# Output norms of a delta rule: the inverse root by Newton steps on GpSimd in place of a logarithm and an exponential on ScalarE

## The chip, the cores and the metric

The kernel runs on one core of one Trainium2 chip. The metric is the time of one execution on the device in microseconds (us), as the median of several runs. A core has five engines that run side by side, each through its own queue in order: TensorE (PE, the matrix multiplications; PEld is its loading of weights), VectorE (DVE), ScalarE (ACT), GpSimd (POOL), and SyncE (SP), whose queue here issues the loads of weights. Matmuls write into PSUM, everything else lies in SBUF.

## The reference, cut to what matters

The model is a trunk of two layers over 256 tokens of width 2048. Layer 0 is differential attention and a gated MLP with a short convolution, layer 1 a gated delta rule and another such MLP. The change lies in layer 1, where the output of the delta rule is normalised for every token and head, multiplied by a gate and projected:

```python
def rms_norm(x, g):
    xf = x.astype(jnp.float32)
    y = xf * lax.rsqrt(jnp.mean(xf * xf, axis=-1, keepdims=True) + RMS_EPS)
    return (y * g.astype(jnp.float32)).astype(x.dtype)

def gated_deltanet(h, w_in, conv_w, a_log, dt_bias, norm_g, w_out):
    ...
    o = gated_delta_rule(q, k, v, g, beta)       # (1, 256, 32 heads, 128)
    o = rms_norm(o, norm_g) * jax.nn.silu(z.reshape(b_sz, s_len, GDN_V_HEADS, GDN_HEAD_DIM).astype(jnp.float32))
    return o.reshape(b_sz, s_len, GDN_VALUE_DIM).astype(h.dtype) @ w_out
```

## The kernel before, in words

**Dense work.** Every projection is done by `dense` (or `dense_tok`, with tokens on the partitions). Weights come in chunks of 512 KB through `weights` (lines 81 to 91): SP issues the load into `raw`, ACT casts it to a rounded high part `whi` (line 89), DVE subtracts to get the low part `wlo` (line 90), and PE multiplies both parts (lines 151 and 152; a third product on line 154 where `wide` is false; lines 220 to 222 in `dense_tok`). Each of the three tiles has four slots. A plain chunk of `dense` is four tiles of the contraction times two tiles of outputs, so eight pairs of matmuls.

**Order of the work.** After each chunk `dense` calls `tick`, which lets every generator in the list `bg` run on to its next `yield`. Small work (keys, inverses, groups) is written as such generators, so that it stands between the chunks in the program. A `yield` means: one chunk later. The framework then plans the order of instructions on each engine over the whole program, with the program's order as priority and a model of their durations; the engines follow the planned queues in order, and semaphores keep the dependencies. Where `issue_after` or `add_manual_dep` stands, the order is bound by hand.

**The delta rule (`gdn`).** Four blocks of four key heads each. A block first projects its keys (`keys`, one generator a head), then one value head, the gates `z` (two calls of `dense_tok`, whose Silu goes into the tiles `zts`), then three more value heads; then comes the output projection of the block before it (`out`, eight calls of `dense` with two chunks each). After the last block its own output projection follows. `invert` and `levels` solve the triangular systems of a block, and for each of two groups of two key heads (four value heads) a generator `group` computes the outputs: so eight groups in all, two a block. Of these, the two of block 0 run while the keys of block 1 are made, and the others beside output projections.

**A group.** PE forms the products with the solved systems (line 773) into PSUM tiles of the pool `mp`, which has four banks. For each half `t` of the tokens an output tile `o` stays in PSUM; ACT squares it (line 796) and DVE adds up the squares for each token and head into `s`, 128 x 8 numbers (tile `os`, line 797). Then `lnexp` puts a load of ScalarE's table for logarithm and exponential on ACT's queue (line 297), bound behind the last sum, and `rsqrt` takes Ln and Exp of `s` (lines 316 and 317). DVE multiplies each `o` by its root and the gate (line 807). Three steps later PE transposes the products (line 818), and ACT and DVE write the high and low parts of `oc` (lines 821 and 822), four tiles of which feed the block's output projection.

**Neighbours.** `keys` uses the same helpers: PE sums its squares with a matrix of ones (line 329), its norms take Ln and Exp of a 128 x 512 tile and four exponentials of the decays, after a table load on line 297; `convs` takes a Silu, which needs another table (loads on line 593). The key step ends in eight copies on GpSimd into the tile `Cc` (line 652), which `invert` of that block reads. PE forms the products of keys and queries on lines 639 and 640 once DVE has scaled them (line 632).

Of the kernel before, what the change touches and what calls it, by code (L numbers as in the profile page):

```python
# [7 lines left out]

F32 = mybir.dt.float32
F32R = mybir.dt.float32r  # L10
AF = mybir.ActivationFunctionType
ALU = mybir.AluOpType
AX = mybir.AxisListType
# [3 lines left out]
P = 128  # L17
T = 256
D = 2048
KD = D // P  # L20
EPS = 1e-6
CK = 4
WARM = 7
LNEXP = "natural_log_exp_and_others"
# [2 lines left out]
class Trunk:  # L27
# [8 lines left out]
    def __init__(self, ctx, tc):  # L36
# [8 lines left out]
        self.mps = ctx.enter_context(tc.tile_pool(name="mps", bufs=4, space=PSUM))  # L45
        self.ones = self.cp.tile([P, P], F32, tag="ones", name="ones")
        nc.vector.memset(self.ones, 1.0)
        self.eps = self.cp.tile([P, 1], F32, tag="eps", name="eps")
        nc.vector.memset(self.eps, EPS)
        self.gx = self.cp.tile([P, KD + KD * T], F32, tag="x", name="x")  # L50
        self.x = self.gx[:, KD:].rearrange("p (k t) -> p k t", t=T)
        self.hs = self.cp.tile([P, KD * 2 * T], F32R, tag="h", name="h")
        self.h = self.rows(self.hs, KD)
        self.onesr = self.cp.tile([P, P], F32R, tag="onesr", name="onesr")
        nc.vector.tensor_copy(self.onesr, self.ones)
# [9 lines left out]
    def mp(self):  # L65
        return self.mps.tile([P, 512], F32, tag="mp", name="mp")

# [8 lines left out]
    def slots(self):  # L76

        return [self.wp.tile([P, CK * T], dt, tag=tag, name=tag, bufs=4)
                for tag, dt in (("raw", F32), ("whi", F32R), ("wlo", F32R))]

    def weights(self, ap, parts=1, slots=None, at=0):
# [5 lines left out]
        for i in range(parts):  # L87
            s = slice(i * n // parts, (i + 1) * n // parts)
            self.cast = nc.scalar.copy(hi[:, :, s], raw[:, :, s])  # L89
            nc.vector.tensor_tensor(lo[:, :, s], raw[:, :, s], hi[:, :, s].bitcast(F32), ALU.subtract)  # L90
        return hi, lo
# [9 lines left out]
    def dense_two(self, w, acts, done):  # L101

        nc = self.nc
        ps = [self.banks(), self.banks()]
        cut = KD - CK
        parts = [(c, (0, 1)) for c in self.firsts() if c[0] < cut] + [((cut, CK), (b,)) for b in range(2)]
        at = 0
# [24 lines left out]
    def dense(self, w, kt, acts, tiles=2, wide=True, each=None, apart=False):  # L132
# [5 lines left out]
        n = 2 * T if wide else T  # L138
        for k0, nk in self.chunks(kt, CK):
            hi, lo = self.weights(w[:, k0:k0 + nk, :])  # L140
# [66 lines left out]
    def dense_tok(self, w, kt, acts):  # L207
# [3 lines left out]
        ps = self.banks()  # L211
        for k0, nk in self.chunks(kt, CK // 2):
            hi, lo = self.weights(w[:, k0:k0 + nk, :])
# [52 lines left out]
    def norm_stat(self, wait=1, pool=None):  # L266
# [17 lines left out]
        m = self.sp.tile([P, T + 2], F32, tag="sq", name="ms", bufs=2)  # L284
        nc.vector.tensor_scalar(m, ps[:, :T + 2], 1.0 / D, EPS, ALU.mult, ALU.add)
        with self.lnexp(last):
# [26 lines left out]
    def rsqrt(self, out, ps, n):  # L313

        nc = self.nc
        nc.scalar.activation(out, ps, AF.Ln, bias=self.eps, scale=1.0 / n)
        nc.scalar.activation(out, out, AF.Exp, scale=-0.5)

    def split(self, out, a):

        self.nc.scalar.copy(out[:, 0], a)
        return self.nc.vector.tensor_tensor(out[:, 1], a, out[:, 0].bitcast(F32), ALU.subtract)
# [42 lines left out]
    def ffn(self, w_up, w_down, nj, cols_ap, done, final=False):  # L365
# [3 lines left out]
        with self.tc.tile_pool(name="fp", bufs=1) as fp:  # L369
# [3 lines left out]
            acts = []  # L373
            rows = self.rows(fp.tile([P, nj * 2 * T], F32R, tag="ac", name="ac"), nj)
            for j in range(nj):
# [17 lines left out]
    def attention(self, w_first, w_qk, w_v, w_o, nh, dist_ap, ident_ap, qg, kg, lvec, sub, start, done, lambda_init):  # L393

        nc, mp = self.nc, self.mp
        with self.tc.tile_pool(name="at", bufs=1) as at:
# [28 lines left out]
            def squares(r):  # L425
                sq = at.tile([P, 2, T], F32, tag="sq", name="sq", bufs=2)
                nc.scalar.square(sq, r)
                sp = at.tile([P, 2, 2, T], F32R, tag="sqp", name="sqp", bufs=3)
                self.split(sp, sq)
# [60 lines left out]
            def values(h, v, aT):  # L490
# [13 lines left out]
                for e in range(2):  # L504
                    on = at.tile([P, T], F32, tag="on", name="on", bufs=2)
                    nc.vector.scalar_tensor_tensor(
                        on, po[:, e * T:(e + 1) * T], subs[:, e:e + 1], ri[:, 0, :], ALU.mult, ALU.mult)
                    ac = at.tile([P, 2, T], F32R, tag=f"ac{h}_{e}", name="ac")
                    self.split(ac, on)
# [32 lines left out]
    def gdn(self, w_gate, w_in, w_z, w_out, nb, hb, gate_ap, const_ap, conv_col, ng, done):  # L542
# [7 lines left out]
        nc, tc, mp = self.nc, self.tc, self.mp  # L550
# [4 lines left out]
        with tc.tile_pool(name="gd", bufs=1) as gd:  # L555
# [204 lines left out]
            def group(gi, gr, lqs, done, vt, ready, zts, acts):  # L760

                TT = TTs[gi]
                n = 2 * len(gr)
                while gi not in done or len(ready) < len(gr):
                    yield
                sub = lqs[2 * gr[0]:2 * gr[-1] + 2]
                yield

                def prod(terms):
                    p = mp().rearrange("p (v c) -> p v c", c=P)  # L770
                    for v in range(n):
                        for i, (l, r) in enumerate(terms):
                            nc.tensor.matmul(p[:, v, :], l(v), r[:, v, :], start=i == 0, stop=i == len(terms) - 1)  # L773
                    return p[:, :n, :]

                w0 = gd.tile([P, gv, P], F32, tag="w0", name="w0", bufs=1)
                w1, r1 = vt[:, 0], vt[:, 1]
                nc.scalar.copy(w0[:, :n, :], prod([(lambda v: TT[:, 2 * v + 1, :], vt[:, 0])]))
                yield
                yield  # L780
                p = prod([(lambda v: sub[v][0][:, T:], w0)])
                nc.vector.tensor_tensor(r1[:, :n, :], r1[:, :n, :], p, ALU.subtract)
                yield
                yield
                nc.scalar.copy(w1[:, :n, :], prod([(lambda v: TT[:, 2 * v, :], r1)]))
                s = gd.tile([P, 2, gv], F32, tag="os", name="os", bufs=2)
                os = []
                for t in range(2):
                    if t == 0:
                        o = prod([(lambda v: sub[v][1][:, P:T], w0)])  # L790
                    else:
                        yield
                        yield
                        o = prod([(lambda v: sub[v][1][:, T:], w0), (lambda v: sub[v][1][:, :P], w1)])
                    sq = gd.tile([P, gv, P], F32, tag="qs", name="osq", bufs=2)
                    nc.scalar.square(sq[:, :n, :], o)
                    last = nc.vector.tensor_reduce(s[:, t, :n], sq[:, :n, :], AX.X, ALU.add)
                    os.append(o)
                with self.lnexp(last):
                    self.rsqrt(s[:, :, :n], s[:, :, :n], P)  # L800
                while gi not in zts:
                    yield
                ys = []
                for t in range(2):
                    y = zts[gi][:, t]
                    for v in range(n):
                        nc.vector.scalar_tensor_tensor(
                            y[:, v, :], os[t][:, v, :], s[:, t, v:v + 1], y[:, v, :], ALU.mult, ALU.mult)
                    ys.append(y)
                yield  # L810
                yield
                yield
                for v0 in range(0, n, 2):
                    p = mp()
                    for i in range(2):
                        for t in range(2):
                            a = i * T + t * P
                            nc.tensor.transpose(p[:, a:a + P], ys[t][:, v0 + i, :], ident)
                    oc = gd.tile([P, 2, 2, T], F32R, tag="oc", name="oc", bufs=hb)
                    pv = p.rearrange("p (v t) -> p v t", v=2)  # L820
                    nc.scalar.mul(oc[:, :, 0, :], pv, ng)
                    nc.vector.scalar_tensor_tensor(
                        oc[:, :, 1, :], pv, ng, oc[:, :, 0, :].bitcast(F32), ALU.mult, ALU.subtract)
                    acts += [oc[:, i] for i in range(2)]
# [10 lines left out]
            for b in range(nb):  # L835
# [5 lines left out]
                for op, i in plan + [("v", i) for i in range(1, hb)]:  # L841
# [7 lines left out]
                    elif op == "z":  # L849
# [3 lines left out]
                        for t in range(2):  # L853
                            nc.scalar.activation(zt[:, t].rearrange(flat), ps[:, t, :], AF.Silu,
                                                 scale=self.rstdc[:, t:t + 1])
# [83 lines left out]
def _layout(inputs):  # L939
# [13 lines left out]
    def blocks(w, kt, starts):  # L953
        w = w.reshape(kt, P, -1)
        return np.stack([np.concatenate([w[:, :, a:a + n] for a, n in s], 2) for s in starts]).transpose(0, 2, 1, 3)
# [25 lines left out]
    qk = blocks(x["diff_w_qkv"][0], KD, [[(T * (h + i), T)] for h in range(NH) for i in (0, NH)])  # L981
    two, cut = qk[:2], KD - CK

# [99 lines left out]
```

## Time and profile before

| what | value |
|---|---|
| runs | 2531.76, 2530.80 and 2531.91 us; median 2531.76 us |
| span of the profiled execution | 2530.1 us, 1.7 us below the median of the runs |
| granted TensorE clock | 1.000 |
| PE busy, PEld busy | 2520.0 and 2309.7 us |
| DVE, ACT, POOL busy | 1908.3, 1513.2 and 103.5 us |
| the stage of the delta rule | about 1060 to 1860 us of the span |

The span runs from the first to the last instruction of one profiled execution. For an engine, busy is the time with an instruction at work; matmuls overlap, so a busy PE is not one at its peak. In rows of the timeline the first number is the start in us from the span's start, the second the time in us that the row covers, then engine, line, operation, tiles (output <- inputs), shape and count; in brackets stands the idle time of the engine before it and what ended it. Rows of a line or tile give the shortest, median and longest duration in ns.

### The profile page before, as it was taken

Reading aid. Unit: us, or ns where it says so; the run is one execution under the profiler, and the core shown is the slowest. Engines: PE = TensorE matmul, PEld = TensorE weight load, DVE = VectorE, ACT = ScalarE, POOL = GpSimd, SP = SyncE. Lnnn points to the kernel's source line nnn. Section 1 sums busy time; section 2 is a strip of 40 time slices with the busy share of each in tenths; the row PEclk is TensorE's granted clock in tenths of the full one; section 3 lists DMA queues with packets and bytes.
Section 4 is the critical chain, followed back from the end, with each engine's and each line's share of the span. In section 5 each row is a group of like instructions: output and inputs, shape, how many; then the busy total and the mean of one; then the engine's idle time right before and its main releaser. Section 6 shows DMA issues by size and latency. Waiting matters only on the chain.

```text
span 2530.1 us, 41598 instructions
## 1 busy us (share of the span) xinstructions
PE 2520.0 (100%) x16151; PEld 2309.7 (91%) x16151; DVE 1908.3 (75%) x2847; ACT 1513.2 (60%) x2098; POOL 103.5 (4%) x197
## 2 busy tenths in 40 slices
PE   9999999999999999999999999999999999999999
PEld 8998899999999999998989989989999999999998
DVE  8886677777777555689788788788887777776544
ACT  7766656666666444485774675675566666665343
POOL 0000000000000000012021021021000000000000
PEclk9999999999999999999999999999999999999999
DMA  7555566666666666666455565555566666666775
GB/s 256 175 184 175 167 203 201 202 202 201 200 201 202 200 200 202 202 187 201 154 185 180 170 188 184 168 175 184 165 201 201 201 201 202 201 201 205 209 207 157
DMA packets 138199, 487.20 MB, mean 193 GB/s; under 512 B 15472, under 2 KB 18448, under 8 KB 138000
## 3 DMA queue, kind: packets, MB, share of 16 engines
q1 hardware_dynamic: 137712, 484.17, 60.8%
q8 instruction: 127, 2.08, 0.3%
q14 instruction: 72, 0.59, 0.1%
q10 hardware_dynamic: 288, 0.35, 0.0%
HBM read 482.32 MB, written 2.15 MB: 191 GB/s over the span
## 4 chain that ended last, share of the span: by engine, by line
PE 95%; ACT 3%; DVE 1%; issue 1%; DMA 0%; SPq 0%; ACTq 0%; DVEq 0%
PE ps L151 51%; PE ps L152 26%; PE ps L221 3%; PE ps L220 3%; PE ps L222 3%; PE mp L773 2%; PE mp L151 1%; PE ps L154 1%; ACT whi L89 1%; PE mp L329 1%; PE mp L152 0%; ACT L593 0%; ACT lt L631 0%; PE ps L123 0%; ACT L297 0%
## 5 line engine op out<-in xcount | busy, mean ns | idle before, releaser
L90 DVE TENSOR_TENSOR wlo<-raw,whi 128x1024 fp32r<-128x1024 f32 (+2 forms) x911 | 1104.1, 1213 | 506.1 <-ACT whi L89 498.2
L89 ACT CAST whi<-raw 128x1024 fp32r<-128x1024 f32 (+2 forms) x911 | 944.2, 1038 | 822.9 <-PE ps L151 657.0
L151 PE MATMUL ps<-h,whi 128*128 128x512 f32 (+1 forms) x4208 | 1369.4, 375 | 0.0
L152 PE MATMUL ps<-h,wlo 128*128 128x256 f32 x4208 | 1151.1, 274 | 1.0 <-DVE wlo L90 1.0
L151 PEld LDWEIGHTS ps<-h,whi 128*128 128x128 f32 x4208 | 796.1, 189 | 102.8
L152 PEld LDWEIGHTS ps<-h,wlo 128*128 128x128 f32 x4208 | 807.7, 192 | 2.8 <-DVE wlo L90 1.3
L151 PE MATMUL ps<-ac,whi 128*128 128x512 f32 x1546 | 506.8, 382 | 0.0
L152 PE MATMUL ps<-ac,wlo 128*128 128x256 f32 x1546 | 421.2, 273 | 0.0
L151 PEld LDWEIGHTS ps<-ac,whi 128*128 128x128 f32 x1546 | 292.1, 189 | 40.8 <-PE ps L151 0.2
L152 PEld LDWEIGHTS ps<-ac,wlo 128*128 128x128 f32 x1546 | 296.8, 192 | 0.1
L151 PE MATMUL ps<-oc,whi 128*128 128x512 f32 x512 | 170.7, 384 | 0.0
L220 PE MATMUL ps<-whi,h 128*128 128x512 f32 x384 | 146.5, 382 | 0.0
L221 PE MATMUL ps<-wlo,h 128*128 128x512 f32 x384 | 146.1, 380 | 0.0
L222 PE MATMUL ps<-whi,h 128*128 128x512 f32 x384 | 145.7, 379 | 0.0
L310 DVE SCALAR_TENSOR_TENSOR cv<-u,fcols,cv 128x255 f32<-128x255 f32 (+1 forms) x344 | 142.9, 477 | 0.0
L152 PE MATMUL ps<-oc,wlo 128*128 128x256 f32 x512 | 142.0, 277 | 0.0
L151 PEld LDWEIGHTS ps<-oc,whi 128*128 128x128 f32 x512 | 96.9, 189 | 12.5
L152 PEld LDWEIGHTS ps<-oc,wlo 128*128 128x128 f32 x512 | 98.3, 192 | 0.5
L308 ACT ACTIVATE cv<-u,fcols 128x256 f32<-128x256 f32 x172 | 93.9, 593 | 0.5 <-DVE u L205 0.5
L343 DVE TENSOR_TENSOR x<-ps,x 128x512 f32<-128x512 f32 x110 | 75.6, 687 | 12.5 <-PE ps L152 11.2
L310 DVE SCALAR_TENSOR_TENSOR cv<-u,cols,cv 128x255 f32<-128x255 f32 (+2 forms) x192 | 84.0, 486 | 0.3
L221 PEld LDWEIGHTS ps<-wlo,h 128*128 128x128 f32 x384 | 72.6, 189 | 10.0 <-DVE wlo L90 0.2
(220 smaller groups left out, 2077.3 us busy)
## 6 DMA issues: line engine op xcount, KB each, us to landing
raw<-w_up SPq DMA_DIRECT2D x344, 512.0 KB, 4.7
raw<-w_down SPq DMA_DIRECT2D x160, 512.0 KB, 3.8
raw<-w_in SPq DMA_DIRECT2D x128, 512.0 KB, 4.7
raw<-w_z SPq DMA_DIRECT2D x64, 512.0 KB, 3.7
raw<-w_out SPq DMA_DIRECT2D x64, 512.0 KB, 4.2
raw<-w_qk SPq DMA_DIRECT2D x56, 512.0 KB, 4.5
raw<-w_v SPq DMA_DIRECT2D x32, 512.0 KB, 3.5
raw<-w_o SPq DMA_DIRECT2D x32, 512.0 KB, 4.7
```

What stands on the lines that cost most here:

```text
L89: self.cast = nc.scalar.copy(hi[:, :, s], raw[:, :, s])
L90: nc.vector.tensor_tensor(lo[:, :, s], raw[:, :, s], hi[:, :, s].bitcast(F32), ALU.subtract)
L151: nc.tensor.matmul(bank[c][:, :n], hi[:, k, s], self.turns(a[:, :n // T, :]), start=first, stop=False)
L152: nc.tensor.matmul(bank[c][:, :T], lo[:, k, s], self.turns(a[:, :1, :]), start=False, stop=last and wide)
L154: nc.tensor.matmul(bank[c][:, :T], hi[:, k, s], self.turns(a[:, 1:, :]), start=False, stop=last)
L220: nc.tensor.matmul(ps[:, c, :], ah, wh, start=first, stop=False)
L221: nc.tensor.matmul(ps[:, c, :], ah, wl, start=False, stop=False)
L222: nc.tensor.matmul(ps[:, c, :], al, wh, start=False, stop=last)
L308: nc.scalar.activation(out, u, AF.Identity, bias=bias, scale=taps[n - 1])
L310: nc.vector.scalar_tensor_tensor(out[:, j:], u[:, :T - j], taps[n - 1 - j], out[:, j:], ALU.mult, ALU.add)
L343: self.nc.vector.tensor_tensor(x, part, x, ALU.add)
L773: nc.tensor.matmul(p[:, v, :], l(v), r[:, v, :], start=i == 0, stop=i == len(terms) - 1)
```

## The change

The group no longer calls `lnexp` and `rsqrt`. DVE forms the mean square plus epsilon, `m`, and a first guess of its inverse root from the bits of `m` read as an integer. Three Newton steps follow, with four operations each, all on GpSimd. The group then yields once before it goes on. The tiles `m`, `y` and `u` are new, 128 x 8 numbers each with two buffers. The row norms and the keys keep `lnexp` and `rsqrt`.

```diff
+I32 = mybir.dt.int32
+ROOT = float(0x5f3759df)
...
+    def root_steps(self, pool, s, scale):
+
+        nc = self.nc
+        m, y, u = (pool.tile(list(s.shape), F32, tag=f"rt{i}", name="rt", bufs=2) for i in range(3))
+        nc.vector.tensor_scalar(m, s, scale, EPS, ALU.mult, ALU.add)
+        nc.vector.tensor_scalar(y.bitcast(I32), m.bitcast(I32), -0.5, ROOT, ALU.mult, ALU.add)
+        for _ in range(3):
+            nc.gpsimd.tensor_tensor(u, y, y, ALU.mult)
+            nc.gpsimd.tensor_tensor(u, u, m, ALU.mult)
+            nc.gpsimd.tensor_scalar(u, u, -0.5, 1.5, ALU.mult, ALU.add)
+            nc.gpsimd.tensor_tensor(y, y, u, ALU.mult)
+        return y
...
-                    last = nc.vector.tensor_reduce(s[:, t, :n], sq[:, :n, :], AX.X, ALU.add)
+                    nc.vector.tensor_reduce(s[:, t, :n], sq[:, :n, :], AX.X, ALU.add)
                     os.append(o)
-                with self.lnexp(last):
-                    self.rsqrt(s[:, :, :n], s[:, :, :n], P)
+                s = self.root_steps(gd, s, 1.0 / P)
+                yield
                 while gi not in zts:
                     yield
```

## The prediction

> **What bounds the kernel now.** I read the page first, then the waits of TensorE, then the group's own tile, then the timelines around the eight groups.
>
> ```profile
> span 2530.1 us, 41598 instructions
> PE 2520.0 (100%) x16151; PEld 2309.7 (91%) x16151; DVE 1908.3 (75%) x2847; ACT 1513.2 (60%) x2098; POOL 103.5 (4%) x197
> PE 95%; ACT 3%; DVE 1%; issue 1%; DMA 0%; SPq 0%; ACTq 0%; DVEq 0%
> ```
>
> TensorE (PE) is busy throughout and is 95% of the chain that ended last; GpSimd (POOL) is nearly idle. The change touches no matmul, so it can move the time only by removing or making waits of PE. Those of the whole delta-rule stage, 1090 to 1855 us (header: engine line waited for, total, times, longest):
>
> ```profile
> PE mp L639 <- DVE cv L632: 1.4, 1, 1.4
> PE ps L152 <- DVE wlo L90: 1.0, 1, 1.0
> PE mp L329 <- ACT qp L321: 0.7, 2, 0.5
> PE mp L329 <- ACT whi L89: 0.5, 1, 0.5
> ```
>
> Together 3.6 us. That is the most a removed wait can give, against 5.06 us, 0.2% of 2531.76, which is about what a measurement of this kernel can tell from no change. Now the rows of the tile of sums `os`, and the table loads of line 297 (one for each norm or key step that takes a logarithm):
>
> ```profile
> L807 DVE SCALAR_TENSOR_TENSOR zt<-mp,os,zt x64: 336/340/351, 1239.2 to 1800.6; 128x128 f32<-128x128 f32 x64
> L316 ACT ACTIVATE os<-os,eps x8: 300/301/302, 1237.7 to 1796.4; 128x8 f32<-128x8 f32 x8
> L317 ACT ACTIVATE os<-os x8: 196/206/209, 1238.0 to 1797.5; 128x8 f32<-128x8 f32 x8
>   ACT os L317: 0.6, 1
> L297 ACT ACT_TABLE_LOAD  x28: 1283/1283/1283, 40.7 to 1860.1; - x28
> ```
>
> Eight groups, each with one load, one Ln and one Exp; their products (L807) found VectorE (DVE) idle for them once, for 0.6 us. Of the 28 loads 16 are the keys', 8 the groups', 4 the row norms'. I number groups (block, group); only (0,0) and (0,1) run beside the next block's keys, the other six beside output projections. The crowded place is (0,1); ACT, then DVE and PE there:
>
> ```profile
> 1258.40 1.28 ACT L297 ACT_TABLE_LOAD   x1 [1.10 <-DVE os L797]
> 1261.18 1.28 ACT L297 ACT_TABLE_LOAD   x1
> 1267.44 1.28 ACT L317 ACT_TABLE_LOAD   x1
> 1268.74 0.63 ACT L317 ACTIVATE qs<-qs 128x512 f32<-128x512 f32 x1
> 1257.69 0.68 DVE L797 TENSOR_REDUCE os<-osq 128x4 f32<-128x512 f32 x1
> 1261.97 2.15 DVE L807 SCALAR_TENSOR_TENSOR zt<-mp,os,zt 128x128 f32<-128x128 f32 x8
> 1264.04 1.21 DVE L90 TENSOR_TENSOR wlo<-raw,whi 128x1024 fp32r<-128x1024 f32 x1
> 1266.93 0.27 PE L152 MATMUL ps<-h,wlo 128*128 128x256 f32 x1
> 1270.14 0.49 PE L639 MATMUL mp<-cv 128*128 128x128 f32 x2 [1.41 <-DVE cv L632]
> ```
>
> PE's longest wait of the stage, 1.41 us, hangs on a key's exponential at 1268.74, behind an ACT queue that the group's load, Ln and Exp stand in.
>
> **The change part by part.** *ACT.* Removed per group: 1.283 + 0.301 + 0.206 = 1.79 us, 14.3 us over eight groups, and at 1258.40 the 1.10 us for which the load held the queue. In seven groups nothing on PE waits for it, so it is worth nothing there: ACT is 60% busy. At (0,1) it lies in the chain of the 1.41 us wait, and just ahead of the 0.5 us wait for a cast; I take both as gone, -1.9 us. Bounds: 0 (the key's own loads at 1261.18 and 1267.44 stay) and -3.6 us (every wait of the stage).
>
> *DVE.* Added: two operations on 128x8 per group, 16 in all. The nearest small row is 128x2:
>
> ```profile
> L476 DVE TENSOR_SCALAR l<-l,nlam 128x2 f32<-128x2 f32 x8 | 1.8, 228 | 0.3
> ```
>
> At 0.23 us each that is 0.46 us per group, 3.7 us in all, hidden under PE at DVE's 75%; uncovered, it is 3.7 us.
>
> *GpSimd.* Added: twelve dependent operations per group, 96 in all. The trace has no arithmetic on POOL; the nearest rows are its copies:
>
> ```profile
> L666 POOL COPY Ti<-half x8: 201/728/1212, 1105.7 to 1551.8; 128x16 f32<-128x16 f32 x8
> 1121.76 3.54 POOL L652 COPY Cc<-lt 32x64 f32<-32x64 f32 x8 [10.20 <-ACT lt L631]
> 1137.35 6.75 POOL L652 COPY Cc<-lt 32x64 f32<-32x64 f32 x8 [12.05 <-ACT whi L89]
> 1138.40 1.25 DVE L90 TENSOR_TENSOR wlo<-raw,whi 128x1024 fp32r<-128x1024 f32 x1
> 1140.22 3.72 DVE L90 TENSOR_TENSOR wlo<-raw,whi 128x1024 fp32r<-128x1024 f32 x3
> 1258.96 3.92 POOL L652 COPY Cc<-lt 32x64 f32<-32x64 f32 x8 [57.42 <-DVE lt L647]
> ```
>
> A small copy takes 0.20 us at its shortest. Eight others take 3.54 us (0.44 each) or, beside four weight subtractions (L90), 6.75 (0.84 each), so DVE's work slows POOL to about twice; L90 itself goes from 1.21 to 1.25. The bounds for a step are therefore 0.20 and 0.84 us, the chain of twelve 2.4 to 10.1 us. I take 0.33: small operands like the 0.20 row, with some of the slowing. Chain 4.0 us, with DVE's part 4.4.
>
> *The step of waiting.* `yield` hands on once, so products, transposes and `oc` come one weight chunk later. A chunk is eight pairs of matmuls; two consecutive pairs start at
>
> ```profile
> 1783.19 0.38 PE L151 MATMUL ps<-oc,whi 128*128 128x512 f32 x1
> 1783.52 0.38 PE L151 MATMUL ps<-oc,whi 128*128 128x512 f32 x1
> 1777.55 0.69 DVE L797 TENSOR_REDUCE os<-osq 128x4 f32<-128x512 f32 x1 [1.41 <-ACT osq L796]
> 1780.74 2.16 DVE L807 SCALAR_TENSOR_TENSOR zt<-mp,os,zt 128x128 f32<-128x128 f32 x8 [0.63 <-ACT os L317]
> 1784.07 0.27 PE L818 MATMUL mp<-con,zt 128*128 128x128 f32 x1
> 1784.01 1.21 DVE L90 TENSOR_TENSOR wlo<-raw,whi 128x1024 fp32r<-128x1024 f32 x1
> 1793.76 0.27 PE L152 MATMUL ps<-oc,wlo 128*128 128x256 f32 x1
> ```
>
> so 8 x 0.33 = 2.6 us. In (3,0) the sums end at 1778.24 and the first transpose starts at 1784.07; without the products that leaves 5.83 - 2.16 = 3.7 us for the root, and one chunk more, 6.3. DVE takes 0.46, so twelve steps fit if one costs under (6.3 - 0.46)/12 = 0.49 us. At 0.33 the six groups beside output projections have 1.9 us to spare: 0. In (0,1) products start 1261.97 - 1258.37 = 3.6 us after the sums; the budget is 6.2 us and the limit 0.48 us. But there POOL also has the eight key copies, from 1258.96 to 1262.88. Behind them the chain starts 4.5 us after the sums and has 1.7 left: it is late by 0.7 us at 0.20 a step, 2.3 at 0.33.
>
> *Who stands behind a late product.* DVE works in order, so L90 stands behind L807, then the cast's slot, then SP's next weight load. Matching each subtraction with the first matmul that reads it (subtractions and chunks in their order), the one at 1264.04 ends 1.7 us before PE reads it at 1266.93; the one at 1784.01 ends 8.5 us before 1793.76. So a late (0,1) costs PE up to 2.3 - 1.7 = 0.6 by this way, and as much again if transposes already queued wait; I charge 1.0, and 0.3 for (0,0), whose ACT and DVE queues are crowded too. Bounds 0 and the 8.2 us of the second rival below. No DMA is issued or moved; SP is touched only through these slots.
>
> *PSUM.* The two output tiles of a group stay one chunk longer in the four-bank pool. No PE wait of the stage is put down to that pool's users L807 or L821; I charge 0, at most one chunk, 2.6 us, once.
>
> Sum: -1.9 + 1.0 + 0.3 = -0.6 us. The profiled span is 2530.1 us, 1.7 below the median of the three times, 2531.76; a difference of spans carries over. Forecast 2531.2 us.
>
> **A rule beside the trace.** The rows of 1137 to 1144 us show copies at 0.84 instead of 0.44 us beside L90. The Trainium skill, "SBUF — State Buffer", section "Who interferes with whom", says that a VectorE instruction with two SBUF inputs contends with a GpSimd instruction that reads SBUF, and that whichever starts first holds the shared ports for its whole instruction. The trace agrees as far as the 0.44 to 0.84 go. By that rule every one of the twelve steps could stand out one whole L90 (1.21 us): an estimate of 12 x (0.20 + 1.21) = 17 us where DVE is never free, far past the budget of 6.3. What speaks against that here: once DVE reaches the product it stands still, and the steps that are left run free. That is the second rival, priced by rows next.
>
> **The rivals.** *The change is hidden altogether*, or the key's loads keep the 1.41 us wait: 2531.8 to 2533, inside the forecast's case.
>
> *Steps at 0.84 us beside the keys (the other side).* In (0,0) sums and products lie so:
>
> ```profile
> 1234.52 0.69 DVE L797 TENSOR_REDUCE os<-osq 128x4 f32<-128x512 f32 x1
> 1239.21 2.16 DVE L807 SCALAR_TENSOR_TENSOR zt<-mp,os,zt 128x128 f32<-128x128 f32 x8
> ```
>
> That is 4.0 us, with the chunk 6.6. The chain is 12 x 0.84 + 0.46 = 10.5 us, so products come 3.9 us late in (0,0) and, against 6.2, 4.3 in (0,1), the key copies not counted. Where PE's in-order queue holds the transposes, that is +8.2 - 1.9 = +6.3: 2538. It decides above 0.48 us a step. For it: the 6.75 us row. Against: DVE's standstill. If all eight groups did so, another 6 x 4.2 = 25 us: 2563; against that stand L90's share beside projections (1.21 of each 2.6 us) and leads of 8.5 us.
>
> *The last block.* Nothing covers block 3 after its group (3,1) but the last projection of block 2. Its transposes and `oc` copies now:
>
> ```profile
> 1803.25 0.60 PE L818 MATMUL mp<-con,zt 128*128 128x128 f32 x4
> 1807.06 0.69 ACT L821 ACTIVATE oc<-mp,cols 128x512 fp32r<-128x512 f32 x1 [0.44 <-PE ps L152]
> 1808.58 0.69 ACT L821 ACTIVATE oc<-mp,cols 128x512 fp32r<-128x512 f32 x1
> ```
>
> The copy at 1807.06 waits for a projection matmul to free its buffer, not for the transposes. These go to 1805.9, still before it. If the copies slip too, PE waits up to one chunk: 2531.2 + 2.6 = 2533.8.
>
> *Faster.* The instruction order is planned over the whole program, and a new order may remove all 3.6 us: 2528.2. Beyond 0.2% it would need waits that the trace doesn't show.
>
> **How the numbers follow.** Forecast 0.70 (2529 to 2533), last block 0.10, steps beside the keys 0.12, all groups late 0.02, faster order 0.03, another order's cost 0.03 (2 slower, 1 faster in 100). Slower by over 0.2% (above 2536.8): 0.12 + 0.02 + 0.02 = 0.16. Faster (under 2526.7): 0.03 + 0.01 = 0.04. Same: 0.80. The range goes from the floor of removable waits, 2528.2, to the second rival, 2538.
>
> **What would show it.** Twenty table loads from the helper on line 297 instead of 28 (line numbers here are those of before). POOL with 96 more instructions, start to start 0.2 to 0.5 us in the six groups, longer in (0,0) and (0,1). PE's wait at L639 near 1270 us gone; if it stands, the ACT step is wrong. DVE idle before L807 put down to POOL: under 1 us beside projections; 2 us or more in most groups, or PE waits at L818, would make the second rival right and the prediction wrong.

## The result, and the profile after

The changed kernel takes 2528.15 us (median of 20 runs, 2527.23 to 2529.39) against 2531.78 us (20 runs, 2530.57 to 2532.68) before: 3.6 us less, ratio 0.9987 with a 95% interval of 0.9981 to 0.9993. The forecast was 2531.2 us, 0.6 us less than before, with a range from 2528.2: the direction and most single steps held, but the gain is six times the forecast and the time lies on the range's lower end. It is 0.85 us under the 2529 to 2533 us to which the prediction gave a chance of 0.70, and at the price of its rival "Faster" (2528.2 us, 0.03), which expected such a time from another order of the instructions.

The page of the changed kernel:

```profile
span 2526.2 us, 41701 instructions
PE 2519.7 (100%) x16151; PEld 2311.8 (92%) x16151; DVE 1909.0 (76%) x2863; ACT 1499.5 (59%) x2074; POOL 130.1 (5%) x293
```

PE's busy time is the same within 0.3 us; the span is 3.9 us shorter, so PE's idle time fell from 10.1 to 6.5 us. ACT lost 13.7 us, POOL gained 26.6 and DVE 0.7. PE's waits in the delta-rule stage, the view shown before:

```profile
PE ps L154 <- DVE wlo L92: 0.5, 1, 0.5
PE mp L654 <- DVE cv L647: 0.4, 1, 0.4
```

(Line numbers move: the products are now line 822, the transposes 833, the key products 654 and 655, the keys' sums 344, subtraction and cast 92 and 91, the table load of `lnexp` 299, the Silu's 608.) The wait for the scaled keys fell from 1.4 to 0.4 us; the three waits at the keys' sums, 0.7 us in two and 0.5 us, are gone. The wait for `wlo` at 1113 us comes before any group. It comes out at 0.4 to 1.1 us in the runs below, whatever was changed.

The rows of the new root (tile `rt`), with what waits for it:

```profile
L328 POOL TENSOR_TENSOR rt<-rt x24: 199/202/1499, 1236.5 to 1794.0; 128x8 f32<-128x8 f32 x24
L330 POOL TENSOR_SCALAR rt<-rt x24: 197/198/1120, 1238.5 to 1795.5; 128x8 f32<-128x8 f32 x24
L326 DVE TENSOR_SCALAR rt<-rt x8: 155/172/173, 1236.3 to 1791.5; 128x8 int32<-128x8 int32 x8
  POOL rt L331: 11.3, 8
```

A step on GpSimd takes 0.20 us in the median, one on DVE 0.17. All eight groups' products wait for GpSimd, 11.3 us in all, and none of it shows as a wait of PE. The table loads of ScalarE, first the helper's and then the Silu's:

```profile
L299 ACT ACT_TABLE_LOAD  x20: 1283/1283/1283, 41.0 to 1856.3; - x20
L608 ACT ACT_TABLE_LOAD  x16: 1283/1283/1283, 1078.9 to 1679.2; - x16
```

The helper's fell from 28 to 20, as the prediction had it. The Silu's fell too; before, the row read

```profile
L593 ACT ACT_TABLE_LOAD  x18: 1283/1283/1283, 1078.6 to 1682.8; - x18
```

and that the prediction had not seen.

Finally the crowded place (0,1), on POOL, DVE and PE in the timeline:

```profile
1262.08 0.20 POOL L328 TENSOR_TENSOR rt<-rt 128x8 f32<-128x8 f32 x1 [0.45 <-DVE rt L326]
1262.35 0.21 POOL L329 TENSOR_TENSOR rt<-rt 128x8 f32<-128x8 f32 x1
1262.65 1.09 POOL L330 TENSOR_SCALAR rt<-rt 128x8 f32<-128x8 f32 x1
1263.82 0.20 POOL L331 TENSOR_TENSOR rt<-rt 128x8 f32<-128x8 f32 x1
...
1266.10 0.20 POOL L331 TENSOR_TENSOR rt<-rt 128x8 f32<-128x8 f32 x1
1262.46 1.23 DVE L92 TENSOR_TENSOR wlo<-raw,whi 128x1024 fp32r<-128x1024 f32 x1 [0.53 <-ACT whi L91]
1266.33 2.16 DVE L822 SCALAR_TENSOR_TENSOR zt<-mp,rt,zt 128x128 f32<-128x128 f32 x8 [2.65 <-POOL rt L331]
1269.14 0.49 PE L654 MATMUL mp<-cv 128*128 128x128 f32 x2 [0.43 <-DVE cv L647]
```

Read the starts: dependent steps follow each other by 0.28 us; one step stood out DVE's weight subtraction (1262.65 to 1263.74, the subtraction ends at 1263.69), then DVE stood at the products and the rest ran free. The chain takes 1266.30 - 1262.08 = 4.2 us, 0.35 a step; over the eight groups it takes 4.2 to 4.8 us, with about one subtraction stood out in each.

### The profile page after: what moved, and what is told of

Read it like the earlier page. It is cut to its first block, busy times and chain, and to the rows that moved or that the text cites. A ratio compares the mean times of both kernels' runs of the same rounds, so it can differ in the third digit from the quotient of the medians.

```text
span 2526.2 us, 41701 instructions
## 1 busy us (share of the span) xinstructions
PE 2519.7 (100%) x16151; PEld 2311.8 (92%) x16151; DVE 1909.0 (76%) x2863; ACT 1499.5 (59%) x2074; POOL 130.1 (5%) x293
## 4 chain that ended last, share of the span: by engine, by line
PE 50%; DVE 0%; issue 0%
PE ps L153 26%; PE ps L154 13%; PE ps L223 2%; PE ps L224 2%; PE ps L222 2%; PE mp L788 1%; PE mp L153 1%; PE ps L156 1%; PE mp L655 0%; PE mp L154 0%; PE mp L753 0%; PE mp L833 0%; PE mp L771 0%; PE mp L654 0%; PE mp L344 0%; PE mp L756 0%
## 5 line engine op out<-in xcount | busy, mean ns | idle before, releaser
L91 ACT CAST whi<-raw 128x1024 fp32r<-128x1024 f32 (+2 forms) x911 | 943.9, 1038 | 844.8 <-PE ps L153 671.0
L153 PE MATMUL ps<-h,whi 128*128 128x512 f32 (+1 forms) x4208 | 1369.6, 376 | 0.0
L153 PEld LDWEIGHTS ps<-h,whi 128*128 128x128 f32 x4208 | 796.1, 189 | 102.9
L153 PE MATMUL ps<-ac,whi 128*128 128x512 f32 x1546 | 506.8, 382 | 0.0
L153 PEld LDWEIGHTS ps<-ac,whi 128*128 128x128 f32 x1546 | 292.1, 189 | 40.6 <-PE ps L153 0.2
L153 PE MATMUL ps<-oc,whi 128*128 128x512 f32 x512 | 170.6, 384 | 0.0
L153 PEld LDWEIGHTS ps<-oc,whi 128*128 128x128 f32 x512 | 96.8, 189 | 12.8
```

What stands on the lines that cost most here:

```text
L153: nc.tensor.matmul(bank[c][:, :n], hi[:, k, s], self.turns(a[:, :n // T, :]), start=first, stop=False)
```

## Experiments

Theory A: the gain is ScalarE's relief. The group's table load, Ln and Exp no longer stand in front of the keys' work. Rival B: the planner lays out another order for any change of the program, and the gain is that order's. Rival C: the step of waiting gives it. For each kernel the table gives the difference of its median from that of the kernel before, run beside it, with the ratio and its 95% interval; single runs of one kernel spread over some 2 us. An interval of 0.0009 to either side is 2.3 us, and the intervals of most of these kernels overlap, so a difference of 1 us between two of them is read only where their traces show it too. Beside it stands a sum that I worked out from each trace: where the start of one matmul follows the last by over 195 ns more than usual for its shape (219 ns for 512 columns, 110 for 256, 112 for 128), between 1060 and 1865 us, the excess is added up ("PE's waits"). The wait at 1113 us, with a small one that stands beside it in some kernels, is in it with 0.6 to 1.8 us. For twelve_steps, whose stage runs past 1865 us, the sum is not given.

| kernel | difference, us | ratio, 95% interval | PE's waits, us |
|---|---|---|---|
| before | 0 | | 4.8 |
| the change | -3.6 | 0.9987 (0.9981 to 0.9993) | 1.3 |
| yield_only | -0.6 | 0.9998 (0.9989 to 1.0007) | 4.2 |
| no_yield | -2.0 | 0.9991 (0.9982 to 0.9999) | 2.6 |
| block0_only | -2.1 | 0.9991 (0.9982 to 1.0000) | 2.9 |
| rest_only | -2.0 | 0.9992 (0.9983 to 1.0001) | 3.5 |
| no_root | -4.6 | 0.9982 (0.9974 to 0.9991) | 1.5 |
| on_vector | -2.9 | 0.9987 (0.9978 to 0.9996) | 2.7 |
| six_steps | +2.9 | 1.0012 (1.0004 to 1.0021) | 8.3 |
| twelve_steps | +76.8 | 1.0303 (1.0289 to 1.0317) | |
| act_back | -1.5 | 0.9993 (0.9984 to 1.0002) | 3.8 |
| load_back | -1.8 | 0.9993 (0.9984 to 1.0002) | 2.5 |
| two_yields | -3.2 | 0.9986 (0.9977 to 0.9995) | 2.0 |
| two_steps | -2.5 | 0.9990 (0.9981 to 0.9999) | 3.2 |

All diffs below are against the changed kernel.

**yield_only**

```diff
-                s = self.root_steps(gd, s, 1.0 / P)
+                with self.lnexp(last):
+                    self.rsqrt(s[:, :, :n], s[:, :, :n], P)
                 yield
```

> The group keeps its table load, Ln and Exp and only yields once more behind them. Theory A (the gain is ScalarE's: the group's load, Ln and Exp no longer stand ahead of a key's exponential beside block 1's keys): no gain, 2531 to 2532.5 us, and PE's wait of 1.4 us for the scaled keys near 1270 us stays. Rival B (any change of the program makes the planner lay out another order, and the gain is that order's): somewhere in 2528 to 2534 us with another set of waits. Rival C (the step of waiting itself relieves VectorE's queue): 2528 to 2529 us.

2530.93 against 2531.48 us, an interval around 1, and 0.07 us under A's range: rival C falls as the sole cause. The 1.4 us wait is gone from this kernel's PE waits too, but another stands in its place, `PE ps L153 <- ACT whi L91` with 1.0 us; theory A had expected the old wait to stay. Another set of waits is what rival B expects.

**no_yield**

```diff
                 s = self.root_steps(gd, s, 1.0 / P)
-                yield
```

> The new root without the step of waiting. Chain on GpSimd 4.3 us as in the changed kernel, against the 3.6 us that stood between sums and products in (0,1) before. A: the ScalarE gain stays, VectorE waits longer for the products (3 us or more in several groups), 2528.5 to 2530.5 us. C: the gain goes, 2531.5 to 2533 us.

2529.47 against 2531.48 us: 2.0 of the 3.6 us stay, as A expects. That the other 1.6 us need the step is not clear of the noise by the times, but without it PE's waits are 2.6 us instead of 1.3, and PE waits 0.8 us for `oc`. VectorE's waits for GpSimd did not grow as expected: they are 0.3 to 3.7 us a group, over 3 us once.

**block0_only and rest_only**

```diff
-                s = self.root_steps(gd, s, 1.0 / P)
-                yield
+                if b == 0:                  # rest_only: if b > 0
+                    s = self.root_steps(gd, s, 1.0 / P)
+                    yield
+                else:
+                    with self.lnexp(last):
+                        self.rsqrt(s[:, :, :n], s[:, :, :n], P)
```

> New root and yield in the two groups of block 0 alone, the old root in the other six. A: the wait near 1270 us falls from 1.4 to 0.4 us or less and the keys' waits right behind it go, 2529.5 to 2530.2 us, about 2 of the 3.6 us. B: any time in 2528 to 2534 us.

> The old root in block 0, new root and yield in the six groups beside output projections. A: the 1.4 us wait near 1270 us stays; 2531 to 2532 us if those groups are worth nothing, as the prediction had it; 2529.5 to 2530.5 us if the other 1.6 us of the gain come from them (waits of the sums of squares in the keys of blocks 2 and 3).

2529.37 and 2529.51 us against 2531.48, the first 0.1 us below A's range, the second in the range given for the case that the six groups have a part in the gain. PE's waits in the stage, block0_only and then rest_only:

```profile
PE ps L154 <- DVE wlo L92: 1.0, 1, 1.0
PE mp L654 <- DVE cv L647: 0.4, 1, 0.4
PE mp L344 <- ACT qp L336: 0.2, 1, 0.2
```

```profile
PE mp L654 <- DVE cv L647: 1.4, 1, 1.4
PE ps L154 <- DVE wlo L92: 1.0, 1, 1.0
PE mp L344 <- ACT whi L91: 0.5, 1, 0.5
```

Block 0 removes the waits near 1270 us (1.4 to 0.4, and the 0.5 for a cast), the other six groups those of the keys' sums for `qp` at 1658 and 1672 us. The wait for `qp` at 1467 us (0.5 in the view before, 0.65 by the starts) goes in both, so the two gains, 2.1 and 2.0 us, count it twice; they add up to 4.1 against 3.6 us.

For rest_only the traces tell the cause apart from rival B. From 1421 to 1578 us and from 1615 to 1686 us, before and rest_only run the same instructions in the same order on PE, ACT, DVE and GpSimd, except for one Silu table load in each stretch (line 593), which rest_only does not have. First before, then rest_only, in the second stretch:

```profile
1626.52 1.05 ACT L89 CAST whi<-raw 128x1024 fp32r<-128x1024 f32 x1 [1.62 <-PE ps L154]
1627.58 1.28 ACT L593 ACT_TABLE_LOAD   x1
1628.88 0.63 ACT L593 ACTIVATE cv<-cv 128x512 f32<-128x512 f32 x1
1672.50 0.48 PE L329 MATMUL mp<-qp,onesr 128*128 128x512 f32 x1 [0.20 <-ACT qp L321]
```

```profile
1625.19 1.05 ACT L91 CAST whi<-raw 128x1024 fp32r<-128x1024 f32 x1 [1.63 <-PE ps L156]
1626.15 0.62 ACT L608 ACTIVATE cv<-cv 128x512 f32<-128x512 f32 x1
1670.07 0.48 PE L344 MATMUL mp<-qp,onesr 128*128 128x512 f32 x1
```

The same matmul starts later in before than in rest_only by 0.56 us from 1217 us, ahead of the first group, up to 1466 us; by 1.32 us from the wait at 1467 to 1644 us; and by 2.43 us from 1672 to 1734 us. So the groups' own loads, Ln and Exp near 1400 and 1600 us cost PE nothing, and the two Silu loads that follow them (1434.2 and 1627.6 us) cost 0.8 and 1.1 us: nearly all of the 2.0 us.

**no_root**

```diff
-                s = self.root_steps(gd, s, 1.0 / P)
                 yield
```

> Leaves the root out: the products take the sums of squares as they are, one step of waiting stays, and neither ScalarE nor GpSimd nor VectorE does anything for the root. This is the whole gain that the removal can give, with nothing put in its place. A (the gain is ScalarE's and GpSimd's chain costs nothing): 2527.5 to 2528.5 us, like the changed kernel. If the chain costs something behind the products (VectorE waited 11.3 us for GpSimd in all): 2525 to 2527 us.

2527.16 against 2531.76 us, between the two expectations. With no root at all the gain is 4.6 us, 1.0 more than with GpSimd's chain. If that is what the chain costs, it is not clear of the noise: the interval of no_root is 2.3 to 6.6 us, that of the change 1.8 to 4.8. Only the wait at 1113 us is left in the view of PE's waits.

**on_vector**

```diff
-            nc.gpsimd.tensor_tensor(u, y, y, ALU.mult)
+            nc.vector.tensor_tensor(u, y, y, ALU.mult)
...                                        # all four operations of a step
```

> The same twelve operations on VectorE, in its queue, with the yield. VectorE gets 96 small operations at 0.17 us, 16 us more busy time, and no wait for GpSimd. A: ScalarE is relieved as before, so 2527.5 to 2529 us. If what matters is work taken off VectorE and ScalarE alike (GpSimd as a free engine): 2529 to 2532 us.

2528.86 against 2531.76 us, within A's range. VectorE's 96 operations of 0.17 us cost no more than can be measured beside GpSimd's chain (0.7 us, within the intervals): the gain does not hang on GpSimd, which is idle otherwise; it comes with ScalarE's relief.

**six_steps and twelve_steps**

```diff
-        for _ in range(3):
+        for _ in range(6):                  # twelve_steps: 12
```

> Six Newton steps, 24 operations on GpSimd, a chain of 24 x 0.35 = 8.5 us against the 6.2 us of the prediction: products 2 us late and more. If the leads of the weight subtractions (5 us and more beside projections) cover it: 2528 to 2529.5 us. If PE's queue stands at the transposes: 8 x 2.2 = 18 us more, 2546 us.

> Twelve Newton steps, 48 operations, 17 us of chain. The planner may lay the products and transposes later; if it does so in full, PE loses at most some 10 us, 2530 to 2540 us. If the queues stand where they stood, products are 11 us late in eight groups, less leads of 2 to 9 us: 2550 to 2600 us.

2534.64 and 2608.57 us. PE's waits of the stage for six steps, the two largest of five:

```profile
PE mp L833 <- DVE zt L822: 2.6, 3, 2.0
PE ps L153 <- DVE oc L837: 2.1, 3, 1.0
```

and for twelve (the first row), with a stretch of its windows (us, busy time of PE, PEld, DVE, ACT and POOL, granted clock, DMA share, GB/s):

```profile
PE mp L833 <- DVE zt L822: 43.8, 9, 12.5
```

```profile
1820.00:1900.00 80.00, 51.62 (x434) 45.47 (x433) 33.83 (x58) 22.17 (x36) 21.85 (x98) 0.81 0.17 57
```

Six steps (chains of 8.5 to 11 us) are past the cover: the transposes wait, and the time is 6.5 us above the changed kernel's, against 18 expected if every group lost its lateness. Twelve (13.5 to 21 us) lose 80 us, more than the highest expectation: besides the 43.8 us of waits the granted clock falls to 0.81 where PE has been waiting. So the second rival of the prediction is real, and three steps lie on the near side of it.

**act_back and load_back**

```diff
+                dead = gd.tile([P, 2, gv], F32, tag="dead", name="dead", bufs=2)
+                with self.lnexp(last):
+                    self.rsqrt(dead, s, P)  # load_back: self.lnexp(last) alone, no dead tile
                 s = self.root_steps(gd, s, 1.0 / P)
                 yield
```

> The changed kernel with ScalarE's old work put back beside it: in every group the table load, the Ln and the Exp run as before, but into a tile that nobody reads; the root still comes from GpSimd. A (the gain is ScalarE's relief): the gain goes, 2530.5 to 2532.5 us. B (the gain is the other order, or the products' later place): stays, 2527.5 to 2529 us.

> The same with the table load alone put back, no Ln and no Exp. The load is 1.28 of the 1.79 us a group, and it waits for the sums at the head of ScalarE's queue. If the load is what cost: 2530 to 2532 us. If the Ln and Exp did: 2528 to 2529 us.

2530.19 and 2529.83 us against 2531.64, each between its two expectations. With ScalarE's old work back, 2.2 of the 3.6 us are lost, and 1.8 of these with the load alone; the 0.4 us between them are within the noise, so Ln and Exp are not shown to cost anything. In load_back the table loads of the helper and of the Silu, and PE's waits, read

```profile
L299 ACT ACT_TABLE_LOAD  x28: 1283/1283/1283, 40.6 to 1857.7; - x28
L608 ACT ACT_TABLE_LOAD  x18: 1283/1283/1283, 1078.4 to 1680.5; - x18
```

```profile
PE ps L153 <- ACT whi L91: 0.9, 1, 0.9
PE ps L154 <- DVE wlo L92: 0.5, 1, 0.5
PE mp L344 <- ACT qp L336: 0.2, 1, 0.2
```

The two Silu loads are back, and so is the wait of the keys' sums for `qp`; near 1268 us PE waits 0.9 us behind a cast. The traces show that the loads do this. From 1231 to 1306 us and from 1615 to 1686 us load_back and the changed kernel have the same order on PE, ACT, DVE and GpSimd, except for the loads: two of the groups' in the first stretch (1235.9 and 1258.6 us), one of the Silu's in the second (1625.2). By the starts of the same matmuls PE falls behind the changed kernel by 0.55 us near 1269 and by 1.2 us between 1642 and 1670: 1.7 us together, where the times differ by 1.8.

Theory A had expected the whole gain to go; 1.5 us stay. The step of waiting alone gives 0.6 (yield_only, not clear of the noise). The wait at 1467 us is gone here too, though the Silu load before it is back (1436.6 us): ACT and PE have another order there than in the kernel before. So some of the rest is the planner's order; how much the products' freedom from ScalarE's queue gives is not settled.

**two_yields and two_steps**

```diff
                 s = self.root_steps(gd, s, 1.0 / P)
                 yield
+                yield                       # two_yields
...
-        for _ in range(3):
+        for _ in range(2):                  # two_steps, without the second yield
```

> The changed kernel with a second step of waiting, so that GpSimd's chain (4.3 us) has 2.6 us more before the products. VectorE's waits for GpSimd, 0.7 to 2.7 us a group, should go. If they cost PE something: 2527 to 2528 us, near the 2527.2 us without a root. If they are covered: 2528 to 2529 us. In the last block the output projection may have to wait for its inputs: up to 2.6 us more, 2531 us.

> Two Newton steps instead of three, eight operations, a chain of 2.9 us, less exact (about 5 parts in a million). With 0 steps 2527.2 and 6 steps 2534.6 us on hand: if the chain's length costs throughout, some 0.3 to 1.0 us below the changed kernel, 2527.2 to 2528 us; if it costs only past the budget of 6.2 us, 2528 to 2528.5 us, the same.

2528.46 and 2529.13 us against 2531.64. With a second step of waiting VectorE still waits 7.8 us for GpSimd, since the planner moves the products up again, and the time is the changed kernel's, as expected if these waits are covered. A shorter chain is no better; both expectations had it at 2528.5 us or less. PE's waits in two_steps, and VectorE in its timeline at (0,1):

```profile
PE ps L154 <- DVE wlo L92: 2.6, 2, 1.5
```

```profile
1261.31 0.16 DVE L326 TENSOR_SCALAR rt<-rt 128x8 int32<-128x8 int32 x1
1263.82 2.16 DVE L822 SCALAR_TENSOR_TENSOR zt<-mp,rt,zt 128x128 f32<-128x128 f32 x8 [2.35 <-POOL rt L331]
1265.90 1.22 DVE L92 TENSOR_TENSOR wlo<-raw,whi 128x1024 fp32r<-128x1024 f32 x1
```

The planner, which counts on a shorter chain, put the products ahead of a weight subtraction that the changed kernel does at 1262.46, before them. VectorE stands 2.35 us for GpSimd, the subtraction stands behind it, and PE waits 1.5 us for `wlo`. So the order of one instruction decides over a microsecond: rival B is real at that size, and single differences of 1 us here are not read further. No version tried beats the changed kernel by what can be measured; the one that leaves the root out is 1.0 us lower, within the intervals.

## Why the prediction was right, and where it was off

*ScalarE at (0,1): -1.9 us.* The waits went as said: the 1.4 us wait fell to 0.4 and the 0.5 us wait went; block0_only gained 2.1 us. That ScalarE's work is the cause of all of it is not shown. By the starts, PE's waits near 1270 us are 2.2 us before, 1.5 in yield_only and act_back, 1.0 in load_back and 0.6 in the changed kernel, so the group's load costs some 0.5 us there, Ln and Exp at most as much again, and 0.8 us went with the step of waiting or another order. The 2.1 us of block0_only also hold the wait at 1467 us, which the prediction did not count here. So the size was right in part by luck.

*ScalarE in the other groups: nothing.* This is the term that was mis-sized: rest_only gained 2.0 us. The prediction looked only at who waits for the group's own load, and the answer was nobody, which rest_only's trace confirms. It missed what the load does to the next one. In the kernel before, ScalarE loads the Silu's table at 1627.58 us, at the start of block 3's keys (shown with rest_only). The last Silu before it was block 2's; between them only the groups' loads at 1586.9 and 1605.2 had changed the table, so the Silu had to load it again. Without the groups' loads that load, and the one at 1434 us for block 2, is not needed: 10 loads go away, not 8. (Two more are placed elsewhere: 55 loads of all kinds become 47.) PE's waits for the keys' sums at 1645, 1658 and 1672 us (0.13, 0.24 and 0.36 us of excess) are gone in the changed kernel, rest_only and no_root, and stand in load_back at 0.14, 0.24 and 0.36. They also stand in yield_only, block0_only and act_back, which keep the groups' loads of block 2, and in none of the kernels without these loads, of which only no_yield has another one there (0.52 us at 1668). No run took the Silu load away alone, but in these stretches before and rest_only, and load_back and the changed kernel, differ by nothing else: the Silu load is the cause.

*The floor of 3.6 us.* Not a floor, though the measured gain equals it. (Nor was it too small to measure: the interval of the change reaches 1.5 us to either side, not 5.) That is luck: 0.9 us of the listed waits still stand in the changed kernel, and the rest of its gain comes from gaps that the list leaves out. no_root gained 4.6. The view of waits counts idle time from the end of a matmul as the profile models it, and lists only the longer ones (the shortest shown here is 0.2 us); the starts of matmuls show 4.8 us of long gaps in the stage before, and 17.7 us in gaps of under 150 ns, which fell to 16.4 in the changed kernel and 15.8 in no_root. The chances did not follow this floor either: the rival "Faster", priced at 2528.2 us, was counted with 0.03 among the times under 2526.7.

*GpSimd's steps: 0.33 us each.* Measured 0.35 to 0.40 (4.2 to 4.8 us for twelve), with 0.28 from start to start where DVE leaves it alone.

*The cost of a late chain: +1.3 us.* 1.0 by no_root, not clear of the noise. In (0,1) GpSimd began 3.1 us after the sums (4.5 said), behind the key copies and DVE's first guess, and the products came 7.3 us after them, 1.1 past the budget of 6.2 (2.3 said). The place was only partly right: DVE waits 0.7 to 2.7 us in every group, not only in block 0, and the leads cover it; the mechanism by which a late product costs PE, a subtraction behind it, is the one that two_steps shows. The "under 1 us beside projections" was passed in two of six groups (1.5 and 1.8 us).

*The step of waiting.* Without it 1.6 us are lost by the times, within the noise, and 1.3 us by PE's waits; so it is worth having. With it the last block's output did not wait.

*The rule on the shared ports.* The measurement decides between its estimate of 17 us and the rows: about one step a chain stood out a whole subtraction (1.09 of the 4.2 us at 1262.65), and eleven did not, because DVE stood at the products. The Trainium skill, "SBUF — State Buffer", section "Who interferes with whom", also has the one that issues first hold the shared ports, in a sentence on VectorE's two-port modes. In the first chain GpSimd's step began at 1236.50, 0.22 us before the subtraction, and still ended only with it:

```profile
1236.50 1.50 POOL L328 TENSOR_TENSOR rt<-rt 128x8 f32<-128x8 f32 x1 [35.09 <-DVE rt L326]
1236.33 0.48 DVE L312 SCALAR_TENSOR_TENSOR cv<-u,cols,cv 128x254 f32<-128x254 f32 x1
1236.72 1.22 DVE L92 TENSOR_TENSOR wlo<-raw,whi 128x1024 fp32r<-128x1024 f32 x1
```

DVE was then already in an operation with two inputs in SBUF (line 312), and its next followed without a gap: GpSimd did not get in between.

## What to carry to other kernels

When an activation on ScalarE that needs another table is taken away, count also the reload that its neighbours no longer need, and look for it at the next use of the other table, even 20 us later. A small chain on an idle engine costs little up to a budget that can be read from the trace (from the operand's end to the consumer's start, less the consumer, plus the steps of waiting); past it the loss grows quickly. Where TensorE is busy all the time, sum the gaps between matmul starts before calling a few named waits the most that can be won. And where two kernels run the same order over a stretch but for one instruction, the lead of one over the other in the starts of the same matmuls tells what that instruction costs.

## What the runs showed of the hardware that was not expected

Operations on 128 x 8 numbers took 0.20 us on GpSimd and 0.17 on VectorE, nearly the same. In the changed kernel 21 steps of GpSimd ran beside nothing on VectorE but operations that take one input from PSUM (lines 358, 598 and 797): all took 0.20 us, as alone. Steps beside the weight subtraction, with both inputs in SBUF, took up to 1.21 us. In twelve_steps the granted TensorE clock was 0.81 in a stretch where PE was busy 51.6 of 80 us. In it, after 12.7 us between two matmul starts, the clock was 0.50 from 1884 to 1889 us, and pairs of matmuls that start every 0.33 us elsewhere started every 0.64 us. So long waits of PE cost more than their own time.
